# An encoder block in split float32: weights' low part last in each K tile, and two low parts per gate and up product made by an accumulating transfer

## The chip, the cores and the metric

The kernel runs on one core of one Trainium2 chip. The metric is the device time of one execution in microseconds (us), the median of several runs. The engines of a core are TensorE (PE, the matmuls; PEld is its loading of weights), VectorE (DVE), ScalarE (ACT), GpSimd (POOL) and SyncE (SP), which issues most of the transfers. Transfers are carried by 16 DMA engines, whoever issues them.

## The reference

One layer of an encoder for 256 tokens of width 2048, all in float32. What matters here is its last part, the feed-forward block, and that all products are matrix products with weights read from HBM once:

```python
x = x + concatenate([out_mla, out_diff]) @ w_out        # two kinds of attention
...
x = x + xo @ w_xo                                        # cross attention
hf = rms_norm(x, g_ffn)
x = x + (silu(hf @ w_gate) * (hf @ w_up)) @ w_down       # 2048 -> 5632 -> 2048
return rms_norm(x, g_final)
```

## The kernel before

**Split float32.** Each float32 operand is held as two parts, high (`.h`) and low (`.l`), in a type that TensorE takes at its fast rate. A product is three matmuls that add into the same accumulator: high by high, high of the activation by low of the weight, low of the activation by high of the weight. The helper `mm` (lines 97 to 101) issues them in this order, at lines 99, 100 and 101. In it the left operand is the activation, which is loaded as TensorE's weights, and the right one is the model's weight, which streams through. `split_into` (line 105) makes the parts of a weight: ScalarE copies the float32 values into `wh`, which rounds them (line 107), and VectorE subtracts the rounded values from the float32 ones into `wl` (line 108).

**Wide products.** `wide_project` (line 254) computes 256 tokens by 1024 columns: two token tiles (`tt`) by two column halves (`oc`), four accumulators of 128x512. The contraction is cut into pairs of K tiles, 256 deep; gate and up have eight pairs (2048 deep). The weights of a pair are one load of 1 MB into a raw buffer `wraw` (`pair_raw`, line 211, issued on SP at line 214, three buffers). A pair is of one of two kinds:

- a plain pair, `P` (lines 270 to 280): two weight blocks of 128x1024, one for each K tile `k`, each split into `wh` and `wl`, and 8 products, 24 matmuls, written in the order `tt`, `oc`, `k`;
- a summed pair, `W` (lines 284 to 318): a scheme with sums of blocks that needs 7 products, 21 matmuls, instead of 8. VectorE forms sums of weight blocks first (`tsum`, lines 287, 291 and 292), which are split as well. Its results go partly to the four accumulators, partly to four more, `Q`.

The split weights have four buffers of 128x1024 for the high and four for the low parts; a plain pair takes two, a summed pair three (and one of another pool). So ScalarE can split at most about two pairs ahead, and then waits for TensorE to be done with the oldest buffer.

For gate and up the kinds are `GU_KINDS = "PPWPWPWP"` (line 39), so that pairs 2, 4 and 6 are summed. The gate product takes the pairs in the order 0 to 7, the up product in the order 0, 2, 1, 4, 3, 6, 5, 7 (line 41). `wide_result` (line 325) runs one such product; the last step, `join` (line 338), adds each accumulator to what the summed pairs gave, on VectorE (line 340). The accumulators and `Q` have four banks each, and change places after every product (line 322). `wide_chunk` (line 901) does gate, SiLU, up and their product for 1024 hidden columns; there are five such chunks (lines 935 to 942), so ten products by `wide_result`. The same `wide_project` also serves the output projection and the down projection (`wide_add`, line 345), and `mm` serves every other product of the kernel.

**Order.** The program gives the order of dependences; which instruction an engine takes next is fixed when the program is built, by a planner that goes through the work with planned times and gives each engine a list. On the chip each engine runs its list in order, and waits where an operand isn't there. Loads by SP are kept in program order. GpSimd's queue carries small arithmetic, four loads of `mem` (line 807) and, at the end, two loads of the last gain (line 952), issued like all its transfers in the order of its list.

Of the kernel before, what the change touches and what calls it, by code (L numbers as in the profile page):

```python
# [15 lines left out]
AF = mybir.ActivationFunctionType  # L16
ALU = mybir.AluOpType
# [4 lines left out]
NT = S // P  # L22
# [14 lines left out]
NPC = (FF - 512) // 1024  # L37

GU_KINDS = "PPWPWPWP"

G_ORDER, U_ORDER = (0, 1, 2, 3, 4, 5, 6, 7), (0, 2, 1, 4, 3, 6, 5, 7)

# [38 lines left out]
def encoder_block(ctx: ExitStack, tc: tile.TileContext, a, out):  # L81
    nc = tc.nc
# [13 lines left out]

    def mm(o, l, r, start, stop, seeded=False):

        nc.tensor.matmul(o, l.h, r.h, start=start, stop=False, skip_group_check=seeded)  # L99
        nc.tensor.matmul(o, l.h, r.l, start=False, stop=False, skip_group_check=seeded)  # L100
        nc.tensor.matmul(o, l.l, r.h, start=False, stop=stop, skip_group_check=seeded)  # L101

    last_split, last_cast = [None], [None]

# [115 lines left out]
        return Split(*[pool.tile([P, 1024], F32R, name=x, tag=x, bufs=bufs)[:, :n * 512].rearrange(  # L220
            "p (b c) -> p b c", b=n) for x in tags])

    def split_blocks(src, pool=None):
        w = w_tile(src.shape[1], pool)
        split_into(w, src)
        return w

    class Pair:
# [22 lines left out]
        split_into(f[:, 4:8, :], s)  # L251
        return Pair(forms=f)

    def wide_project(pairs, src, order, kinds, leave, join, closed=(0, 1), before=None, seed=None):

        accs = [[acc_tile() for _ in range(2)] for _ in range(NT)]
        used = [[seed is not None] * 2 for _ in range(NT)]
# [7 lines left out]
        for n, i in enumerate(order):  # L265
# [2 lines left out]
                before(n)  # L268
            raw = pair_raw(src[i])
            if i not in summed:  # L270
                w = [split_blocks(raw[:, 2 * k:2 * k + 2, :]) for k in range(2)]
                for tt in range(NT):
                    for oc in range(2):
                        for k in range(2):

                            ends = stop or i == plain[-1] and tt == oc == 1
                            mm(accs[tt][oc], pairs[i].at(k, tt), w[k][:, oc, :], not used[tt][oc],
                               ends and k == 1 and oc in closed, seed is not None)
                            used[tt][oc] = True
                continue  # L280
            if i == summed[0]:
                Q = {q: ps_tile(f"q{q}") for q in (1, 5, 7, 6)}
# [24 lines left out]
            own = i == summed[0], i == summed[-1]  # L307
            t1, t3, t2, t4 = [t[:, j, :] for t in (t13, t24) for j in range(2)] if sum_pool else t13 + t24
            A11, A12, A21, A22, S5, S6, S7, S3 = [pairs[i].forms[:, n, :] for n in range(8)]
            mm(Q[1], A11, b11[:, 0, :], *own)  # L310
            mm(accs[0][1], S3, b11[:, 1, :], False, stop, seed is not None)
            mm(Q[5], S5, t1, *own)
            mm(Q[7], S7, t3, *own)
            mm(accs[0][0], A12, b21[:, 0, :], False, stop, seed is not None)
            mm(Q[6], S6, t2, *own)
            mm(accs[1][0], A22, t4, False, stop, seed is not None)
            if i == summed[-1]:
                leave(Q)
        for tt in range(NT):
# [5 lines left out]
    def wide_result(pairs, src, order, kinds):  # L325

        res = []

        def leave(Q):
            res[:] = [act.tile([P, 2, 512], F32, name=f"res{tt}", tag="act") for tt in range(NT)]  # L330
            q1, x, v, y = res[0][:, 0, :], res[0][:, 1, :], res[1][:, 0, :], res[1][:, 1, :]
            nc.scalar.copy(out=q1, in_=Q[1])
            nc.vector.tensor_tensor(out=v, in0=Q[6], in1=q1, op=ALU.subtract)
            nc.vector.tensor_tensor(out=x, in0=Q[5], in1=v, op=ALU.add)
            nc.vector.tensor_tensor(out=v, in0=v, in1=Q[7], op=ALU.subtract)
            nc.vector.tensor_tensor(out=y, in0=Q[5], in1=v, op=ALU.add)

        def join(tt, oc, acc):
            r = res[tt][:, oc, :]
            nc.vector.tensor_tensor(out=r, in0=acc, in1=r, op=ALU.subtract if (tt, oc) == (1, 0) else ALU.add)  # L340

        wide_project(pairs, src, order, kinds, leave, join)
        return res

    def wide_add(pairs, src, order, kinds, oc0, done=None, closed=(0, 1), before=None):
# [744 lines left out]
```

## Time and profile before

| | |
|---|---|
| median of 3 runs | 1142.07 us (1141.78 to 1142.09) |
| the profiled execution's own time | 1141.65 us |
| its span, first to last instruction | 1139.8 us |
| granted TensorE clock | 0.998 |
| instructions | 14403, of them 5390 matmuls |

The profile is of one execution. Its page has the busy time of each engine; the groups of instructions by line, with count, busy time, mean duration and the idle time ahead of them with what ended it; and the DMA queues. The trace behind it answers further views: waits (engine, line and tile that waited, `<-`, what it waited for, then the sum in us, the number of times and the longest), stretches of time with each engine's busy time, a timeline (start, duration, engine, line, operation, out<-in, shape, and in brackets the idle time before and what ended it), and for a line its instructions and the time from a transfer's issue to its landing, as shortest, median and longest. A matmul's shown duration of 0.39 us is longer than the distance to the next one, since matmuls overlap in the array; the distance between starts is its price.

### The profile page before, as it was taken

The page shows a single profiled execution, that of the slowest core. Times are in us where ns is not written, and L with a number is a line of the kernel's source. Part 1 is how long each engine was busy: PE and PEld are TensorE (multiplying, and loading weights), DVE is VectorE, ACT ScalarE, POOL GpSimd, SP SyncE. Part 2 cuts the span into 40 slices and gives each one's busy share as a digit, 9 for nine tenths or more (in the row PEclk, how much of TensorE's full clock was granted, in tenths as well). Part 3 has the DMA queues.
Part 4 walks back from the last instruction along what each step waited for, and adds up shares of the span by engine and source line. Part 5 has one row for each costly group of instructions (what it writes and reads, how often), then busy time and mean ns, then how long its engine had stood idle before and what let it go on. Part 6 is the DMA issues. An engine that isn't in the chain of part 4 may idle for free.

```text
span 1139.8 us, 14403 instructions
## 1 busy us (share of the span) xinstructions
PE 1130.6 (99%) x5390; PEld 946.4 (83%) x5390; DVE 973.2 (85%) x1322; ACT 667.5 (59%) x965; POOL 58.6 (5%) x75
## 2 busy tenths in 40 slices
PE   9999999999999999999999999999999999999997
PEld 7888888888788888888888888888888888888886
DVE  7788766878896777989898988998998898999895
ACT  7755455567566555665565555565554564665663
POOL 5910000000001000000000000000000000000000
PEclk9999999999999999999999999999999999999999
DMA  9655333546567444455556556556555555565553
GB/s 362 241 195 185 124 125 139 181 149 224 191 227 259 156 161 179 161 211 189 212 194 219 185 191 218 185 190 216 185 187 220 201 205 190 191 247 196 195 181 129
DMA packets 35494, 222.13 MB, mean 195 GB/s; under 512 B 4321, under 2 KB 5601, under 8 KB 11105
## 3 DMA queue, kind: packets, MB, share of 16 engines
q1 hardware_dynamic: 33696, 216.60, 52.9%
q0 software_dynamic: 864, 3.15, 0.8%
q10 hardware_dynamic: 864, 1.47, 0.4%
q8 instruction: 42, 0.69, 0.2%
q14 instruction: 28, 0.22, 0.1%
HBM read 219.11 MB, written 2.10 MB: 194 GB/s over the span
## 4 chain that ended last, share of the span: by engine, by line
PE 98%; issue 1%; ACT 0%; DVE 0%; POOLq 0%; POOL 0%; ACTq 0%
PE acc L99 26%; PE acc L101 26%; PE acc L100 26%; PE q L100 4%; PE q L99 4%; PE q L101 4%; PE pt L502 2%; PE ppt L650 1%; PE psc L100 1%; PE psc L101 1%; PE psc L99 1%; PE acckv L99 0%; PE acckv L101 0%; PE acckv L100 0%; PE pt L922 0%
## 5 line engine op out<-in xcount | busy, mean ns | idle before, releaser
L107 ACT CAST wh<-wraw 128x1024 fp32r<-128x1024 f32 (+2 forms) x401 | 389.8, 989 | 283.2 <-PE acc L101 219.5
L108 DVE TENSOR_TENSOR wl<-wraw,wh 128x1024 fp32r<-128x1024 f32 (+2 forms) x401 | 455.3, 1148 | 88.8 <-ACT wh L107 86.8
L107 ACT CAST wh<-tsum 128x1024 fp32r<-128x1024 f32 (+1 forms) x98 | 98.0, 1006 | 73.1 <-PE acc L101 29.7
L108 DVE TENSOR_TENSOR wl<-tsum,wh 128x1024 fp32r<-128x1024 f32 (+1 forms) x98 | 113.6, 1165 | 19.5 <-ACT wh L107 19.5
L100 PE MATMUL acc<-wl,x2n_h 128*128 128x512 f32 x320 | 124.5, 390 | 0.0
L101 PE MATMUL acc<-wh,x2n_l 128*128 128x512 f32 x320 | 123.9, 389 | 0.0
L99 PE MATMUL acc<-wh,x2n_h 128*128 128x512 f32 x320 | 108.2, 390 | 0.0
L100 PE MATMUL acc<-wl,x0T_h 128*128 128x512 f32 x224 | 88.5, 395 | 0.0
L101 PE MATMUL acc<-wh,x0T_l 128*128 128x512 f32 x224 | 88.2, 394 | 0.0
L99 PE MATMUL acc<-wh,x0T_h 128*128 128x512 f32 x224 | 86.9, 396 | 0.0
L100 PE MATMUL q<-wl,forms_h 128*128 128x512 f32 x191 | 74.3, 389 | 0.0
L101 PE MATMUL q<-wh,forms_l 128*128 128x512 f32 x191 | 74.1, 389 | 0.0
L100 PE MATMUL acc<-wl,hT_h 128*128 128x512 f32 x188 | 73.3, 392 | 0.0
L101 PE MATMUL acc<-wh,hT_l 128*128 128x512 f32 x188 | 72.4, 389 | 0.0
L101 PEld LDWEIGHTS acc<-wh,x2n_l 128*128 128x128 f32 x320 | 60.1, 188 | 12.4
L100 PEld LDWEIGHTS acc<-wl,x2n_h 128*128 128x128 f32 x320 | 60.1, 188 | 12.3
L99 PEld LDWEIGHTS acc<-wh,x2n_h 128*128 128x128 f32 x320 | 59.9, 188 | 12.3
L99 PE MATMUL q<-wh,forms_h 128*128 128x512 f32 x191 | 66.7, 389 | 0.0
L99 PE MATMUL acc<-wh,hT_h 128*128 128x512 f32 x188 | 64.5, 391 | 0.0
L100 PE MATMUL acc<-wl,forms_h 128*128 128x512 f32 x162 | 62.5, 389 | 0.0
L101 PE MATMUL acc<-wh,forms_l 128*128 128x512 f32 x162 | 62.4, 389 | 0.0
L99 PE MATMUL acc<-wh,forms_h 128*128 128x512 f32 x162 | 61.3, 389 | 0.0
(402 smaller groups left out, 2247.9 us busy)
## 6 DMA issues: line engine op xcount, KB each, us to landing
wraw<-in_w_gate SPq DMA_DIRECT2D x44, 1024.0 KB, 4.8
wraw<-in_w_up SPq DMA_DIRECT2D x44, 1024.0 KB, 4.8
wraw<-in_w_dn SPq DMA_DIRECT2D x41, 1024.0 KB, 4.8
wraw<-in_w_in SPq DMA_DIRECT2D x24, 1024.0 KB, 4.8
wraw<-in_w_out SPq DMA_DIRECT2D x16, 1024.0 KB, 4.8
wraw<-in_w_in_lat SPq DMA_DIRECT2D x5, 832.0 KB, 7.2
wraw<-in_w_xk SPq DMA_DIRECT2D x4, 1024.0 KB, 5.4
wraw<-in_w_xq SPq DMA_DIRECT2D x4, 1024.0 KB, 5.9
```

Of the source, the lines that this page charges most:

```text
L99: nc.tensor.matmul(o, l.h, r.h, start=start, stop=False, skip_group_check=seeded)
L100: nc.tensor.matmul(o, l.h, r.l, start=False, stop=False, skip_group_check=seeded)
L101: nc.tensor.matmul(o, l.l, r.h, start=False, stop=stop, skip_group_check=seeded)
L107: last_cast[0] = nc.scalar.copy(out=dst.h, in_=src).ins
L108: last_split[0] = nc.vector.tensor_tensor(out=dst.l, in0=src, in1=dst.h.bitcast(F32), op=ALU.subtract).ins
L502: nc.tensor.transpose(out=pt[:, j * P:(j + 1) * P], in_=src[:, j * P:(j + 1) * P], identity=ident)
L650: nc.tensor.transpose(out=pt[:, kt * S + tt * P:kt * S + (tt + 1) * P], in_=p[:, tt, kt * P:(kt + 1) * P], identity=ident)
```

## The change

Two things are changed. First, the three matmuls of a product now come as high by high, low of the activation by high of the weight, and then high of the activation by low of the weight. A new helper `mm_late` does this for several products at once: for all of them the first two matmuls, and then for all of them the last one. In a plain pair it gets the four products of one K tile at a time, so that `k` is now the outer loop; in a summed pair it gets groups of two, and one single product.

Second, in the gate and up products the second block (`k == 1`) of pairs 1 and 5 gets its low part in another way. ScalarE writes the negated rounded values into `wl` and the rounded values into `wh`; then GpSimd issues a transfer from the raw weights (in SBUF) onto `wl` that adds what it brings to what is there. VectorE's subtraction isn't done for these blocks.

```diff
+GU_CARRIED = (1, 5)
...
     def mm(o, l, r, start, stop, seeded=False):
-        nc.tensor.matmul(o, l.h, r.h, start=start, stop=False, skip_group_check=seeded)
-        nc.tensor.matmul(o, l.h, r.l, start=False, stop=False, skip_group_check=seeded)
-        nc.tensor.matmul(o, l.l, r.h, start=False, stop=stop, skip_group_check=seeded)
+        mm_late([(o, l, r, start, stop)], seeded)
+
+    def mm_late(products, seeded=False):
+        for o, l, r, start, stop in products:
+            nc.tensor.matmul(o, l.h, r.h, start=start, stop=False, skip_group_check=seeded)
+            nc.tensor.matmul(o, l.l, r.h, start=False, stop=False, skip_group_check=seeded)
+        for o, l, r, start, stop in products:
+            nc.tensor.matmul(o, l.h, r.l, start=False, stop=stop, skip_group_check=seeded)
...
-    def split_blocks(src, pool=None):
+    def split_blocks(src, pool=None, by_transfer=False):
         w = w_tile(src.shape[1], pool)
-        split_into(w, src)
+        if by_transfer:
+            nc.scalar.activation(w.l, src, AF.Copy, scale=-1.0)
+            last_cast[0] = nc.scalar.copy(out=w.h, in_=src).ins
+            nc.gpsimd.dma_start(out=w.l, in_=src, accum_op=ALU.add)
+        else:
+            split_into(w, src)
         return w
...
-                w = [split_blocks(raw[:, 2 * k:2 * k + 2, :]) for k in range(2)]
-                for tt in range(NT):
-                    for oc in range(2):
-                        for k in range(2):
+                w = [split_blocks(raw[:, 2 * k:2 * k + 2, :], by_transfer=k == 1 and i in carried) for k in range(2)]
+                for k in range(2):
+                    products = []
+                    for tt in range(NT):
+                        for oc in range(2):
                             ends = stop or i == plain[-1] and tt == oc == 1
-                            mm(accs[tt][oc], pairs[i].at(k, tt), w[k][:, oc, :], not used[tt][oc],
-                               ends and k == 1 and oc in closed, seed is not None)
+                            products.append((accs[tt][oc], pairs[i].at(k, tt), w[k][:, oc, :], not used[tt][oc],
+                                             ends and k == 1 and oc in closed))
                             used[tt][oc] = True
+                    mm_late(products, seed is not None)
                 continue
...
-            mm(Q[1], A11, b11[:, 0, :], *own)
-            mm(accs[0][1], S3, b11[:, 1, :], False, stop, seed is not None)
-            mm(Q[5], S5, t1, *own)
-            mm(Q[7], S7, t3, *own)
-            mm(accs[0][0], A12, b21[:, 0, :], False, stop, seed is not None)
-            mm(Q[6], S6, t2, *own)
-            mm(accs[1][0], A22, t4, False, stop, seed is not None)
+            seeded = seed is not None
+            mm_late([(Q[1], A11, b11[:, 0, :], *own), (accs[0][1], S3, b11[:, 1, :], False, stop)], seeded)
+            mm_late([(Q[5], S5, t1, *own), (Q[7], S7, t3, *own)], seeded)
+            mm(accs[0][0], A12, b21[:, 0, :], False, stop, seeded)
+            mm_late([(Q[6], S6, t2, *own), (accs[1][0], A22, t4, False, stop)], seeded)
...
-        wide_project(pairs, src, order, kinds, leave, join)
+        wide_project(pairs, src, order, kinds, leave, join, carried=GU_CARRIED)
```

More of the change, by code (lines that the diff above doesn't have):

```diff
@@ L252, in summed_pair, with wide_project @@
         return Pair(forms=f)
-    def wide_project(pairs, src, order, kinds, leave, join, closed=(0, 1), before=None, seed=None):
+    def wide_project(pairs, src, order, kinds, leave, join, closed=(0, 1), before=None, seed=None, carried=()):
         accs = [[acc_tile() for _ in range(2)] for _ in range(NT)]
```

## The prediction

> **What bounds the kernel now.** I read the page's totals first, then the waits of TensorE, then the busy time of the gate and up stage, because the transfers that the change adds all lie there.
>
> ```profile
> span 1139.8 us, 14403 instructions
> ...
> PE 1130.6 (99%) x5390; PEld 946.4 (83%) x5390; DVE 973.2 (85%) x1322; ACT 667.5 (59%) x965; POOL 58.6 (5%) x75
> ...
> q1 hardware_dynamic: 33696, 216.60, 52.9%
> q0 software_dynamic: 864, 3.15, 0.8%
> ```
>
> TensorE is busy in all but 9.2 us of the span. A busy TensorE can still stand still for a moment, so the waits have to be seen. The view of waits, for TensorE alone, has three rows in all:
>
> ```profile
> PE wps L384 <- DVE warm L378: 1.2, 1, 1.2
> PE acc L99 <- ACT acc L261: 0.8, 1, 0.8
> PE po L99 <- ACT val_h L113: 0.2, 1, 0.2
> ```
>
> The first is ahead of the warm-up at the very start. In the work proper TensorE waits 0.8 + 0.2 = 1.0 us, and never for a low part of a weight. The busy time by stages says where the other idle time is:
>
> ```profile
> core 0: us, PE busy (x) PEld busy (x) DVE busy (x) ACT busy (x) POOL busy (x), PEclk, DMA share, GB/s
> 436.00:1030.00 594.00, 594.00 (x2662) 492.15 (x2661) 538.57 (x643) 343.05 (x414) 1.53 (x3) 1.00 0.56 200
> 1030.00:1140.00 110.00, 102.78 (x496) 86.48 (x494) 91.31 (x122) 58.14 (x80) 1.12 (x2) 0.98 0.48 172
> ```
>
> From 436 to 1030 us, which holds all gate and up products, TensorE is busy 594.00 of 594.00 us at the full clock. The other 7.2 us (110 less 102.78) are the tail after the last matmul. VectorE is busy 538.57 of the 594, ScalarE 343.05, and neither is waited for. The pace of the matmuls closes the account. These are the first matmul of one gate pair's 24 and the first of the next pair:
>
> ```profile
> 703.18 0.39 PE L99 MATMUL acc<-wh,oddh 128*128 128x512 f32 x1
> ...
> 708.62 0.39 PE L99 MATMUL acc<-wh,x2n_h 128*128 128x512 f32 x1
> ```
>
> 5.44 us for 24 matmuls is 0.227 us each, one behind the other. So the kernel is bound by the number of its matmuls, and the change leaves that number as it is. What can be gained is the 1.0 us of waits; what can be lost is any wait that is put into a stage that has none.
>
> **The change part by part.** *Order of the matmuls.* High by high, low of the activation by high, and only then high by low of the weight; and in plain pairs the first K tile of all four accumulators before the second. The number of matmuls and weight loads stays. A low part is needed later, which spares waits that the view doesn't show: 0, with -1.0 to 0 as bounds; I take -0.3. The order makes all four accumulators of a last plain pair finish in its last four matmuls, 0.9 us, where the written order let one finish every six, 1.36 us apart, so the first joins start up to 4.1 us later. Four joins at 0.68 us are 2.7 us of VectorE; the banks are wanted again by the next product's first summed pair, at the earliest one plain pair (5.4 us) later. That covers it.
>
> *Work removed from VectorE, added to ScalarE.* Five wide chunks, gate and up, two pairs each: 20 subtractions go, 20 negating copies come.
>
> ```profile
> L108 DVE TENSOR_TENSOR wl<-wraw,wh 128x1024 fp32r<-128x1024 f32 x334 | 403.9, 1222 | 78.0 <-ACT wh L107 76.3
> L107 ACT CAST wh<-wraw 128x1024 fp32r<-128x1024 f32 x334 | 345.8, 1052 | 238.1 <-PE acc L101 185.4 <-issue 23.7 <-PE q L101 8.7
> ...
> L340 DVE TENSOR_TENSOR res<-acc,res 128x512 f32<-128x512 f32 x40 | 26.3, 682 | 0.4 <-PE acc L101 0.4
> ```
>
> VectorE loses 20 x 1.22 = 24.4 us. TensorE never waits for it, so that is worth 0. ScalarE gets 20 x 1.05 = 21 us more, and it stands idle for 185.4 us before these casts alone, until TensorE frees a weight buffer. It works in order, so casts behind a negation come 1.05 us later. For an up product's pair 5, these are pair 7's casts:
>
> ```profile
> 675.37 1.99 ACT L107 CAST wh<-wraw 128x1024 fp32r<-128x1024 f32 x2
> ...
> 693.91 1.05 ACT L107 CAST wh<-wraw 128x1024 fp32r<-128x1024 f32 x1 [1.06 <-PE acc L101]
> ...
> 695.34 2.95 ACT L107 CAST wh<-wraw 128x1024 fp32r<-128x1024 f32 x3
> ```
>
> The three casts from 695.34 are pair 5's second block and pair 7's two. They end at 698.29, would end at 699.34, and pair 7's matmuls begin at 703.18: 3.8 us of cover, cost 0.
>
> *The transfer.* This is the term that decides. GpSimd issues it when the negation is done, here at about 695.34 + 1.05 = 696.4. Its low part is wanted by the last four matmuls of the pair, which ends where pair 7 begins, at 703.18; four matmuls before that stands this row (the one above it is used further down):
>
> ```profile
> 691.17 0.84 PE L99 MATMUL q<-wh,forms_h 128*128 128x512 f32 x3
> ...
> 702.28 0.39 PE L100 MATMUL acc<-wl,x2n_h 128*128 128x512 f32 x1
> ```
>
> So it has from 696.4 to 702.28, 5.9 us. That the negation can't start much sooner is seen in the bracket on the cast at 693.91: ScalarE stands waiting for a buffer that TensorE still reads. No accumulating transfer is in the trace. The nearest rows are the two plain loads of the same size, 512 KB, on the same queue (line 807 and line 952):
>
> ```profile
> L807 POOL DMA_DIRECT2D mn<-in_mem x4: 537/543/790, 347.5 to 349.4; - x4
> ...
> DMA to landing us min/median/max: 4.9/6.6/10.1
> ```
>
> ```profile
> L952 POOLq EVENT_SEMAPHORE  x2: 17/21316/42616, 435.7 to 1015.8; - x2
> ...
> DMA to landing us min/median/max: 6.9/7.2/7.6
> ```
>
> Each row is of several loads that share the queue (the four go out within 1.9 us of each other, and 10.1 is the last of them); a carried transfer goes alone, so the shortest, 4.9 us, is nearest, and it reads the on-chip memory instead of HBM. The floor is 512 KB on SP's queue, 3.5 us:
>
> ```profile
> wraw<-in_w_down SPq DMA_DIRECT2D x6, 512.0 KB, 3.5
> ```
>
> Against it: the destination has to be read as well, and weights come in beside it (52.9% of the DMA engines' time). Queue 0's 864 packets for six 512 KB loads took 0.8% of 16 engines, 146 us, which is 144 packets, 9 an engine, and 1.5 us an engine for one load. I take 4.9 and half of that 1.5 more for the second reading, 5.6 us: 0.3 us early. Bounds: 3.5 to 7.6, thus 2.4 early to 1.7 late; early is worth nothing, late costs 0 to 1.7 x 20 = 34 us. The order of TensorE's matmuls is fixed when the program is built, by planned times; it can put other pairs' matmuls ahead of the four, which would widen the 5.9 us, but on the chip it can't change.
>
> By the Trainium skill ("DMA: Bandwidth & Descriptors", section "Anatomy of one DMA — SWDGE (gpsimd) path") such a transfer costs 2.0 us and its bytes at 436 GB/s, an estimate of 3.2 us for 512 KB. By that it would be 2.7 us early; the trace's rows are above it, 4.9 at the least, and they are what the sum uses.
>
> *Issue.* 20 x 0.54 = 11 us on GpSimd, which is busy 58.6 us. The load of line 952 sits at the head of its queue from 435.7 to 1015.8, waiting; the transfers come ahead of it in the program and have to be issued in that time, so that it waits behind them costs nothing before 1015. 20 transfers add 10 MB to 222, 20 MB with the destination's reading.
>
> *The raw buffer.* A transfer reads the raw weights until it lands, and the load three later needs that buffer. SP waits for just this kind of release, a low part's subtraction:
>
> ```profile
> SPq L214 <- DVE wl L108: 645.0, 127, 11.5
> ```
>
> Pair 1 of the same up product:
>
> ```profile
> 678.50 0.33 SPq L214 DMA_DIRECT2D wraw<-in_w_up  x1
> ```
>
> ```profile
> 677.25 1.22 DVE L108 TENSOR_TENSOR wl<-wraw,wh 128x1024 fp32r<-128x1024 f32 x1
> ...
> 685.94 1.22 DVE L287 TENSOR_TENSOR tsum<-wraw 128x1024 f32<-128x1024 f32 x1
> ```
>
> The subtraction ends at 678.47, the load goes at 678.50, and with
>
> ```profile
> wraw<-in_w_up SPq DMA_DIRECT2D x44, 1024.0 KB, 4.8
> ```
>
> it lands at 683.3; its first reader runs at 685.94, 2.6 us later. Pair 1's second cast ran at 675.37 (the negation would take its place, and the transfer go at 676.4), so at 5.6 us the transfer lands at 682.0, the load goes 3.5 us later than 678.50 and its reader is 0.9 us late. From the reader's start a sum (1.22) and a cast (1.05) lead to 688.2; TensorE takes up that summed pair first at 691.17. The 2.9 us between hide the 0.9: cost 0. At 7.6 us the reader is 2.9 us late, just covered. Loads queued on SP behind the held one are held too, by less.
>
> Sum, against the profiled execution's own 1141.65 us (span 1139.8 and 1.85 around it): -0.3 + 0 = 1141.3. That run lies 0.4 under the median of 1142.07, so the forecast for the median is **1141.8 us**, no change that a measurement of this kernel could tell (0.2%, 2.3 us).
>
> **The rivals.** *A, forecast:* transfers land in time. Own range 1140.5 (all waits gone, and 0.5 of scatter) to 1144.3 (a few land a tenth late).
>
> *B, slower: the low part comes late.* The place is the last four matmuls of pairs 1 and 5; it decides from 5.9 us on. For it: but for the 4.9, every time in the two rows is over 5.9. Against: those shared their queue, and the order may have been planned with other matmuls between. At 6.6 us it costs 0.7 x 20 = 14 us, 1156; at 7.6, 34 us, 1176.
>
> *C, slower: every byte is read twice.* The transfer reads source and destination through the same engines, so its 1.5 us an engine doubles: 4.9 + 1.5 = 6.4 at best, up to 7.6 + 1.5 = 9.1, and is 0.5 to 3.2 us late, 10 to 64 us; likeliest near the lower end, 0.65 us late, 13 us, 1155. The Trainium skill says that such an add needs two source reads and pushes twice the traffic through the read ring ("Collectives: The Full Stack", section "The bandwidth ceiling: the fold count and why AG ≠ RS ≠ AR"). No run here shows it yet.
>
> *D, slower: the held raw buffer.* The place is the sums of gate pair 4 and up pair 6, whose load needs the buffer of pair 1; it decides from a transfer of 7.6 us on. At 9.1 us the reader is 4.4 us late against 2.9 of cover, 1.5 us in 10 of the 20 cases, 15 us, 1157. It comes only along with B or C, so little is left for it alone.
>
> *E, faster:* the new order changes the pace of the matmuls, or saves at the start and the tail. 1% of TensorE's 1130.6 us would be 11 us. Against: the trace has the three kinds in several orders, and the pace is 0.227 through all of the 24 above.
>
> **How the numbers follow.** A 0.50, B 0.24, C 0.18, D 0.03, E 0.05. Faster is E, 0.05; same is A, 0.50; slower is B, C and D, 0.45. Likeliest is A, 1141.8. The range begins at A's 1140.5 and goes up to 1164, over B's middle (1159) and C's lower half; left out are E, B's top quarter and C's upper part, about 0.2.
>
> **What would show it.** Right: TensorE's waits stay near 1 us, no row in which its matmuls at the new line for the low part wait for a DMA onto wl, VectorE about 24 us less busy, ScalarE 21 more, 20 transfers on queue 0 landing within 5.9 us of their issue. Wrong by B or C: a row of PE waiting for a DMA onto wl, near 20 times, and landing times above 5.9. Wrong by D: VectorE's sums at the line of tsum waiting for raw weights for more than the few us of now, with TensorE waiting behind. Wrong altogether: gains in stages where TensorE had no wait.

## The result, and the profile after

The changed kernel takes **1153.03 us** (median of 4 runs, 1150.71 to 1154.26), against 1142.08 for the kernel before on the same chip: a ratio of 1.0094, 95% interval 1.0076 to 1.0111. That is 10.9 us slower, where the forecast was no change. The two kernels' runs don't overlap. The time lies inside the range, 2 to 3 us under the likeliest prices of rivals B (1156) and C (1155), but, as the runs below show, mostly for another reason than either.

The totals of the page after (the profiled execution took 1152.62 us):

```profile
span 1150.8 us, 14749 instructions
...
PE 1134.9 (99%) x5390; PEld 947.0 (82%) x5390; DVE 950.3 (83%) x1302; ACT 684.1 (59%) x985; POOL 75.5 (7%) x95
...
q0 software_dynamic: 3744, 13.63, 5.7%
```

The work moved as forecast: the same 5390 matmuls, VectorE 22.9 us less busy, ScalarE 16.6 more (the page counts overlapping instructions once; its 20 copies alone add up to 21.1), 10 MB more on queue 0. TensorE is 4.3 us more "busy" though it does the same, and the span has grown by 11.0: so it both waits more and, somewhere, runs slower. The view of waits for TensorE, all of its rows:

```profile
PE q L106 <- ACT forms_h L115: 2.8, 1, 2.8
PE acc L106 <- ACT wh L115: 2.2, 4, 0.7
PE wps L397 <- DVE warm L391: 1.2, 1, 1.2
PE po L107 <- DVE val_l L122: 1.1, 2, 0.8
PE acc L109 <- DVE wl L116: 0.4, 1, 0.4
PE acc L109 <- DMA wl<-wraw: 0.3, 1, 0.3
PE po L106 <- ACT val_h L121: 0.2, 1, 0.2
```

Leaving the warm-up out, 1.0 us of waits has become 7.0. The surprise is what leads the list. A DMA onto `wl`, which rivals B and C named, is next to last. The longest wait is a single one, for `forms_h`: the activation of a summed pair, in a down product, where no transfer was added. And `val_l` (line 122) belongs to the cross attention, where the change touches nothing but the order of three matmuls.

What follows that longest wait, in the timeline of TensorE:

```profile
583.66 0.39 PE L109 MATMUL acc<-wl,forms_h 128*128 128x512 f32 x1
586.86 0.50 PE L106 MATMUL q<-wh,forms_h 128*128 128x512 f32 x1 [2.81 <-ACT forms_h L115]
...
588.12 0.63 PE L109 MATMUL q<-wl,forms_h 128*128 128x512 f32 x1
588.55 0.63 PE L106 MATMUL q<-wh,forms_h 128*128 128x512 f32 x1
```

From 587.7 to 590.7 the starts are 0.43 us apart instead of 0.227. The busy time by stretches shows why; the third figure from the right is the granted clock:

```profile
580.00:583.60 3.60, 3.60 (x17) 2.98 (x16) 3.60 (x7) 1.86 (x3) 0.00 (x0) 1.00 0.18 30
587.50:590.70 3.20, 3.20 (x10) 2.44 (x9) 1.77 (x2) 2.09 (x2) 0.00 (x0) 0.51 0.82 317
592.00:600.00 8.00, 8.00 (x37) 6.64 (x36) 6.48 (x8) 5.39 (x7) 0.00 (x0) 1.00 0.53 200
```

After the wait the clock stood at half for 3.4 us (the trace's clock records have it from 587.6 to 591.0). So this one wait costs its 3.0 us and 1.7 more. By the Trainium skill ("TensorE: Matmul & The Clock Gate", section "What's actually happening") the clock falls to half after an idle window of about 3.4 us, counted freely, and comes back after as much busy time; the trace agrees with the half and, by these 3.4 us, with the way back, but here 2.8 us of idle time were enough.

Adding up, over all matmuls, how far the distance to the next start exceeds 0.227 us gives 22.1 us after and 12.9 before; the 9.2 between them is most of the loss. By places, after less before:

- 4.7 us at this wait;
- 1.7 at 1068 to 1075 us, behind VectorE's `wl` and `hT_l`;
- 1.7 at two waits for ScalarE's `wh` (762 and 1016 us);
- 1.2 at three waits for the DMA onto `wl` (961, 999 and 1048 us; two of them are too short for a row of the view above);
- 1.2 in the cross attention (403 to 407 us) and 0.4 in the memory projection (328 us);
- 0.7 in the first nine microseconds, long before the first transfer (481 us).

Against these stands 1.0 at 288 us, the prediction's wait for `acc`, which is gone; all other places together have 1.3 less than before.

The transfers themselves, by the view of line 236:

```profile
L236 POOL DMA_DIRECT2D wl<-wraw x20: 854/862/933, 481.2 to 1042.9; - x20
...
DMA to landing us min/median/max: 4.5/4.5/5.5
```

They landed in 4.5 us, at worst 5.5, inside the 5.9 us that were reckoned to be there. But 5.9 was worked out at one place of the 20. Where TensorE stood for a transfer, the low part was wanted sooner: 4.3 us after the issue at 961 us, 4.1 at 999 and 5.4 at 1048.

**Where the long wait comes from.** `forms_h` is made from the product of gate and up. The last four matmuls of an up product, the joins of the four accumulators and the first transposes, here from the timeline of before:

```profile
558.71 1.29 DVE L340 TENSOR_TENSOR res<-acc,res 128x512 f32<-128x512 f32 x2 [0.36 <-PE acc L101]
...
561.00 0.39 PE L101 MATMUL acc<-wh,oddl 128*128 128x512 f32 x1
...
564.86 0.60 PE L502 MATMUL pt<-ident,res 128*128 128x128 f32 x4
...
581.39 0.37 ACT L107 CAST forms_h<-pt 128x256 fp32r<-128x256 f32 x1 [0.67 <-DVE sums L248]
```

and here from the timeline after:

```profile
561.42 1.07 PE L109 MATMUL acc<-wl,oddh 128*128 128x512 f32 x4
...
562.50 2.48 DVE L353 TENSOR_TENSOR res<-acc,res 128x512 f32<-128x512 f32 x4
...
569.36 0.60 PE L515 MATMUL pt<-ident,res 128*128 128x128 f32 x4
...
586.43 0.37 ACT L115 CAST forms_h<-pt 128x256 fp32r<-128x256 f32 x1 [1.64 <-DVE sums L261]
```

The last matmul of the product starts at 561.00 before and at 561.42 + 3 x 0.227 = 562.10 after, so the changed kernel is 1.1 us behind at this point. But its four accumulators are all finished by that one group of four matmuls, so the four joins run in one block from 562.50, 3.8 us later than the first one did before, 2.7 of them not from being behind; the transposes come 4.5 us later, the forms 5.0 (3.9 of them new; the 1.2 beyond the joins' 2.7 arise between joins and forms, and I haven't traced them), and the down product stands.

**Where the late `wl` and `hT_l` come from.** The last transfer took longest, 5.5 us from 1042.92, and landed at 1048.43. SP waited 9.9 us for it, the longest single wait in this row, and sent the load of raw weights that needed its buffer at 1048.57:

```profile
SPq L222 <- DMA wl<-wraw: 164.3, 20, 9.9
```

ScalarE stood for that load and VectorE behind ScalarE; from 1056.60 to 1074.30 VectorE was then busy for 17.62 of 17.70 us, among other things with the block of four joins, and TensorE stood for it:

```profile
1055.49 2.00 ACT L115 CAST wh<-wraw 128x1024 fp32r<-128x1024 f32 x2 [4.92 <-DMA wraw<-in_w_dn]
1056.57 1.23 DVE L116 TENSOR_TENSOR wl<-wraw,wh 128x1024 fp32r<-128x1024 f32 x1 [5.49 <-ACT wh L115]
1070.30 0.49 PE L109 MATMUL acc<-wl,forms_h 128*128 128x512 f32 x1 [0.40 <-DVE wl L116]
```

This is rival D's mechanism, a raw buffer held by a transfer, with a place and a size of its own: the loads behind the last transfer, and 1.7 us.

### The profile page after: what moved, and what is told of

It is laid out like the page before. It is cut to its first block, busy times and chain, and to the rows that moved or that the text cites. A ratio compares the mean times of both kernels' runs of the same rounds, so it can differ in the third digit from the quotient of the medians.

```text
span 1150.8 us, 14749 instructions
## 1 busy us (share of the span) xinstructions
PE 1134.9 (99%) x5390; PEld 947.0 (82%) x5390; DVE 950.3 (83%) x1302; ACT 684.1 (59%) x985; POOL 75.5 (7%) x95
## 4 chain that ended last, share of the span: by engine, by line
PE 86%; DMA 4%; DVE 4%; issue 4%; ACT 1%; SPq 0%; POOLq 0%; POOL 0%; ACTq 0%; DVEq 0%
PE acc L106 23%; PE acc L109 23%; PE acc L107 23%; PE q L107 3%; PE q L106 3%; PE q L109 3%; DVE wl L116 2%; PE pt L515 2%; DMA wl<-wraw 1%; DMA wraw<-in_w_up 1%; DMA wraw<-in_w_dn 1%; PE ppt L663 1%; PE psc L109 1%; PE psc L107 1%; PE psc L106 1%
## 5 line engine op out<-in xcount | busy, mean ns | idle before, releaser
L116 DVE TENSOR_TENSOR wl<-wraw,wh 128x1024 fp32r<-128x1024 f32 (+2 forms) x381 | 431.4, 1145 | 125.9 <-ACT wh L115 102.4
L115 ACT CAST wh<-wraw 128x1024 fp32r<-128x1024 f32 (+2 forms) x381 | 369.5, 985 | 250.9 <-PE acc L107 163.6
L106 PE MATMUL acc<-wh,x2n_h 128*128 128x512 f32 x320 | 125.1, 391 | 0.0
L109 PE MATMUL acc<-wl,x2n_h 128*128 128x512 f32 x320 | 94.0, 391 | 0.4 <-DMA wl<-wraw 0.3
L106 PE MATMUL q<-wh,forms_h 128*128 128x512 f32 x191 | 74.7, 392 | 2.9 <-ACT forms_h L115 2.8
L106 PE MATMUL acc<-wh,hT_h 128*128 128x512 f32 x188 | 72.6, 391 | 0.0
L109 PE MATMUL q<-wl,forms_h 128*128 128x512 f32 x191 | 69.6, 392 | 0.0
L302 DVE TENSOR_TENSOR tsum<-wraw 128x1024 f32<-128x1024 f32 x44 | 53.7, 1220 | 5.6 <-DMA wraw<-in_w_up 2.7
```

Of the source, the lines that this page charges most:

```text
L109: nc.tensor.matmul(o, l.h, r.l, start=False, stop=stop, skip_group_check=seeded)
L115: last_cast[0] = nc.scalar.copy(out=dst.h, in_=src).ins
L116: last_split[0] = nc.vector.tensor_tensor(out=dst.l, in0=src, in1=dst.h.bitcast(F32), op=ALU.subtract).ins
L302: nc.vector.tensor_tensor(out=t[:, 0:2, :], in0=raw[:, 1:3, :], in1=raw[:, 0:1, :].to_broadcast([P, 2, 512]), op=ALU.add)
```

## The experiments

The theory after this reading: most of the loss comes from the order of the matmuls, by two details of it (accumulators that finish together, and the activation's low part being wanted second), and the transfers add a smaller part. The rival: the transfers are what costs, directly, by the raw buffer that they hold, or by ScalarE's copies. The kernel before ran beside each experiment and took 1141.95 to 1142.22 us.

**1. The order alone.** The new order everywhere, no transfers.

```diff
-GU_CARRIED = (1, 5)
+GU_CARRIED = ()
```

> All of the new order of matmuls, no transfer: VectorE makes all low parts again. Order theory (the loss of 11 us comes from the order: accumulators of a plain pair all finish in its last four matmuls, so joins, the product of gate and up, the transposes and the forms of the down product come later, and TensorE waits for forms_h near the down products): 1150 to 1153 us, with the 3 us wait for forms_h still there. Transfer theory (low parts, casts and loads delayed by the transfers): 1141 to 1143 us, and no wait of TensorE over 1 us. If both parts have a share, between 1144 and 1149.

Measured: 1148.72 us (1145.88 to 1149.08), ratio 1.0053 (1.0038 to 1.0068). Its waits of TensorE without the warm-up and `val_h`:

```profile
PE q L106 <- ACT forms_h L115: 2.9, 1, 2.9
...
PE po L107 <- DVE val_l L122: 1.1, 2, 0.8
PE acc L106 <- ACT wh L115: 0.5, 1, 0.5
```

The order alone costs 6.6 us, inside what was expected if order and transfers both have a share, with the waits for `forms_h` and `val_l` of the changed kernel; the transfers are left with 1153.0 - 1148.7 = 4.3. The waits behind VectorE at 1068 to 1075 us are not there, nor is there a row of ScalarE waiting for raw weights of gate, up or `in_w_dn`. The profiled execution took 1145.88 us, and in it the clock stayed at 1.00 through the 3 us after the `forms_h` wait, at a mean of 0.999; the other three took 1148.6 to 1149.1 at a mean of 0.996 to 0.997. So the half clock seems to come after this wait in some executions and not in others; only the profiled ones show it directly.

**2. The transfers alone.** The order of before, in all products, with the 20 transfers.

```diff
-                w = [split_blocks(raw[:, 2 * k:2 * k + 2, :]) for k in range(2)]
+                w = [split_blocks(raw[:, 2 * k:2 * k + 2, :], by_transfer=k == 1 and i in carried) for k in range(2)]
                 for tt in range(NT):
                     for oc in range(2):
                         for k in range(2):
```

> The kernel before with its own order of matmuls, and the 20 transfers. Order theory: 1142 to 1143 us, since a transfer lands in 4.5 us and the time it has is 5.9; at most the 0.9 us of waits for transfers that the changed kernel shows. Transfer theory: 1149 us or more, rather above the changed kernel, since the low part is wanted earlier in a pair. Only-together theory: 1142 to 1143 here and in the run with the order alone.

Measured: 1169.56 us (1168.4 to 1170.2), ratio 1.024 (1.0223 to 1.0257). The first rows of TensorE's waits, and the transfers:

```profile
PE acc L102 <- DMA wl<-wraw: 12.9, 11, 2.2
PE q L101 <- ACT forms_h L109: 2.8, 2, 1.8
```

```profile
wl<-wraw POOLq DMA_DIRECT2D x20, 512.0 KB, 4.5
```

The order theory's 1142 to 1143 fell. Here is the wait that rivals B and C described: the transfers take the same 4.5 us in the median, but the low part is wanted by the fifth matmul of the pair instead of the last four. So the two halves of the change belong together: without the late order the transfers cost 27 us. The waits in these two rows come to 15.7 of the 27; three stretches of 3.4 us at half the clock add some 5, and I have not accounted for the rest row by row.

**3. and 4. The two parts of the order.** First, without transfers, only the three matmuls of a product turned round, with loops and grouping as before:

```diff
         nc.tensor.matmul(o, l.h, r.h, start=start, stop=False, skip_group_check=seeded)
-        nc.tensor.matmul(o, l.h, r.l, start=False, stop=False, skip_group_check=seeded)
-        nc.tensor.matmul(o, l.l, r.h, start=False, stop=stop, skip_group_check=seeded)
+        nc.tensor.matmul(o, l.l, r.h, start=False, stop=False, skip_group_check=seeded)
+        nc.tensor.matmul(o, l.h, r.l, start=False, stop=stop, skip_group_check=seeded)
```

> Only the three matmuls of each product in the new order (high by high, low of the activation by high, high by low of the weight), for every product of the kernel; the loops of a plain pair as before (token tile, column half, K tile), no grouping, no transfers. Order theory with the loops as the cause: 1141.5 to 1142.5 us, accumulators finish one by one. If the order of the three is the cause: 1147 to 1153. Transfer theory: 1142.

Measured: 1144.4 us (1143.56 to 1145.48), ratio 1.002 (1.0011 to 1.003), with the wait for `val_l` and none for `forms_h`. Then only the loops of a plain pair turned round, K tile outermost, with the three matmuls as before:

```diff
-                for tt in range(NT):
-                    for oc in range(2):
-                        for k in range(2):
+                for k in range(2):
+                    for tt in range(NT):
+                        for oc in range(2):
```

> Only the loops of a plain pair changed, K tile outermost; the three matmuls of a product in the old order, no grouping, no transfers. Order theory with the loops as the cause: 1147 to 1153 us, with a wait of TensorE for forms near the first down product. If the order of the three or the grouping is the cause: 1141.5 to 1142.5. Transfer theory: 1142.

Measured: 1145.1 us (1144.11 to 1146.97), ratio 1.0028 (1.0016 to 1.004). Here the longest wait is the other one, and `val_l` is gone from the list:

```profile
PE q L99 <- ACT forms_h L107: 2.5, 1, 2.5
```

Each half of the order has its own wait. Both times lie between the two values that had been expected, since neither half is the whole cause: 2.3 and 3.0 us make 5.3 of the 6.6.

**5. and 6. Mending one detail at a time in the changed kernel.** First the end of a product: its last pair goes in the loops of before, one product at a time; all else, transfers too, as in the changed kernel.

```diff
-                for k in range(2):
-                    products = []
-                    for tt in range(NT):
-                        for oc in range(2):
...
-                    mm_late(products, seed is not None)
+                places = [(k, tt, oc) for k in range(2) for tt in range(NT) for oc in range(2)]
+                if stop:
+                    places = [(k, tt, oc) for tt in range(NT) for oc in range(2) for k in range(2)]
...
+                for n0 in range(0, 8, 1 if stop else 4):
+                    mm_late(products[n0:n0 + (1 if stop else 4)], seed is not None)
```

> The changed kernel, but in the last pair of each wide product the loops are as before (token tile, column half, K tile), one product at a time, so that accumulators finish one by one. Late-accumulator theory: the 3 us wait for forms_h near the first down product goes, and with it up to 1.6 us of half clock behind it: 1147.5 to 1150.5 us. Rival (any reordering of matmuls costs this much, wherever the accumulators end): 1152 to 1155, with the wait there or at another place.

Measured: 1147.47 us (1145.87 to 1147.94), ratio 1.0045 (1.003 to 1.006). The wait for `forms_h` has left the list, and 5.6 of the 10.9 us with it. The waits behind VectorE at 1068 to 1075 us are gone as well, though ScalarE waits 5.2 us for the held load here too: three of the four joins run before it, and no longer in one block behind it. Then, instead, single products (the helper `mm`) in the order of before, groups as in the changed kernel:

```diff
     def mm(o, l, r, start, stop, seeded=False):
-        mm_late([(o, l, r, start, stop)], seeded)
+        nc.tensor.matmul(o, l.h, r.h, start=start, stop=False, skip_group_check=seeded)
+        nc.tensor.matmul(o, l.h, r.l, start=False, stop=False, skip_group_check=seeded)
+        nc.tensor.matmul(o, l.l, r.h, start=False, stop=stop, skip_group_check=seeded)
```

> The changed kernel, but every single product (attention, projections by pieces, one product of each summed pair) has its three matmuls in the old order; only the grouped ones have the low part of the weight last. Theory: the attention's output products, whose left operand's low part is wanted second instead of third, lose 1.3 us near 404 us and the memory projection 0.3: 1151 to 1152 us, with the waits for val_l there gone. Rival (the place is planned by chance): 1153 and the waits stay or move.

Measured: 1150.9 us (1150.17 to 1152.42), ratio 1.008 (1.0065 to 1.0095): 2.1 us come back, and `val_l` has left the list, as has the 0.4 in the memory projection. (The two kernels' runs overlap; runs 7 and 12 give 2.2 for the same edit without transfers, where they don't.) Why that wait arises is seen in the cross attention. The product with the values is called with `val` as the left operand, so the reversed order wants `val_l` second instead of third. Before:

```profile
404.80 0.28 PE L99 MATMUL po<-pxT_h,val_h 128*128 128x256 f32 x1
404.92 0.28 PE L100 MATMUL po<-pxT_l,val_h 128*128 128x256 f32 x1
405.24 0.39 PE L101 MATMUL po<-pxT_h,val_l 128*128 128x256 f32 x1
```

After:

```profile
404.27 0.50 PE L106 MATMUL po<-pxT_h,val_h 128*128 128x256 f32 x2 [0.16 <-ACT val_h L121]
405.06 0.39 PE L107 MATMUL po<-pxT_h,val_l 128*128 128x256 f32 x1 [0.28 <-DVE val_l L122]
...
405.79 0.50 PE L106 MATMUL po<-pxT_h,val_h 128*128 128x256 f32 x2
407.12 0.38 PE L107 MATMUL po<-pxT_h,val_l 128*128 128x256 f32 x1 [0.83 <-DVE val_l L122]
```

**7. Both details mended, no transfers.** What is left of the change is the grouping: weights' low parts last in each K tile of all wide products, but for their last pair.

> The last two edits together, and no transfer. If late accumulators and the order of single products are all that the order costs: 1141.5 to 1143.5 us. If grouping as such costs as well: 1145 to 1148.

Measured: 1141.8 us (1141.6 to 1142.33, 10 runs), ratio 0.9999 (0.999 to 1.0008). The order's whole cost is gone. Neither does the grouping gain anything.

**8. The transfer reads HBM instead of the raw buffer.** In the changed kernel, so that no transfer holds a raw buffer.

```diff
-            nc.gpsimd.dma_start(out=w.l, in_=src, accum_op=ALU.add)
+            nc.gpsimd.dma_start(out=w.l, in_=by_transfer, accum_op=ALU.add)
...
-                w = [split_blocks(raw[:, 2 * k:2 * k + 2, :], by_transfer=k == 1 and i in carried) for k in range(2)]
+                w = [split_blocks(raw[:, 2 * k:2 * k + 2, :], by_transfer=src[i][:, 2:4, :] if k == 1 and i in carried else None) for k in range(2)]
```

> The changed kernel, but the transfer reads the raw weights from HBM a second time, instead of from the raw buffer; the buffer is free as soon as ScalarE has read it. Held-buffer theory (the 4.3 us that the transfers add to the order come from loads of raw weights issued about 4 us later): 1148 to 1150.5 us, SP waits for wl transfers gone, ScalarE no longer waiting for raw weights of up, gate and down. Rival (they come from transfers' own lateness, or from ScalarE's 20 more copies): 1152 to 1155, above the changed kernel if reading HBM makes the transfer slower.

Measured: 1194.58 us (1186.99 to 1196.72), ratio 1.0447 (1.0405 to 1.0488). The expectation for the held buffer fell; what came is what the rival had named at its end, a slower transfer: this edit changes the transfer's own time far more than the buffer. Its transfers, and the leading waits of TensorE:

```profile
wl<-in_w_gate POOLq DMA_DIRECT2D x10, 512.0 KB, 8.3
wl<-in_w_up POOLq DMA_DIRECT2D x10, 512.0 KB, 8.4
```

```profile
PE acc L109 <- DMA wl<-in_w_up: 26.2, 10, 5.5
PE acc L109 <- DMA wl<-in_w_gate: 6.3, 7, 2.1
```

So it answers nothing about the held buffer, but it tests the 5.9 us: landing after 8.3 to 8.4 is 2.4 to 2.5 too late, which 20 times makes 48 to 50 us by rival B's sum; against the changed kernel it lost 41.6. That this is near is in part luck. The two rows hold 17 waits of 32.5 us in all, and half the clock for 23.9 us of the span gives some 12 more. Taking each wait off its transfer's time to landing, the low part was wanted 5.3 to 7.1 us after the issue in the up products and 6.3 or more in the gate products. So the point from which a transfer is late was about right for the up products, and too early for the gate ones.

**9. Both details mended, transfers kept.** Single products as in run 6, the last pair of a product as in run 5.

> The changed kernel with both edits at once: the last pair of each wide product one product at a time, and single products in the written order of before; the 20 transfers stay. Without the transfers this order takes 1141.8 us. If order and transfers cost independently of each other, the transfers leave what they added before (1153.0 - 1148.7 = 4.3 us): 1146.1, and 1150.9 - (1153.0 - 1147.5) = 1145.4 by the two other runs. If most of what the transfers cost comes only by way of the waits that the order makes (a long wait of TensorE and the slower matmuls behind it), it is 1142.5 to 1144. The view of waits tells which: a DMA onto wl, or ScalarE's and VectorE's wh and wl behind a raw buffer that came late.

Measured: 1143.92 us (1143.46 to 1145.0, 11 runs), ratio 1.0017 (1.0008 to 1.0026). Its waits of TensorE without the warm-up and `val_h`:

```profile
PE acc L101 <- ACT wh L117: 1.0, 2, 0.5
PE acc L111 <- DMA wl<-wraw: 0.9, 1, 0.9
```

The transfers cost 2.1 us over run 7 (1.9 when each is taken against the kernel before that ran beside it), half of the 4.3 that they cost in the changed kernel: the two parts are not independent, as the second expectation had it. Of the two waits for `wh`, one lies at 7.5 us, before any transfer, and the other is run 7's. In this kernel the one wait for a DMA belongs to the one transfer that took longest, 6.2 us, the last, which shares queue 0 with the loads of the last gain. With two shorter ones (535 and 702 us) the distances at waits for the DMA are 1.6 us too long, so in this execution the late low part is most of what can be seen. ScalarE still waits 4.9 us for the held load, as in the changed kernel, but here TensorE never stands behind it.

**10. The negated copies alone.** As run 9, but the low parts are VectorE's, and nothing uses ScalarE's 20 copies.

```diff
         if by_transfer:
             nc.scalar.activation(w.l, src, AF.Copy, scale=-1.0)
-            last_cast[0] = nc.scalar.copy(out=w.h, in_=src).ins
-            nc.gpsimd.dma_start(out=w.l, in_=src, accum_op=ALU.add)
-        else:
-            split_into(w, src)
+        split_into(w, src)
```

> As the last, but the low parts are VectorE's subtraction again and no transfer is issued; ScalarE still writes the 20 negated copies, which nothing uses. Theory that the transfers cost by their lateness or by the raw buffer that they hold: no loss here, 1141.5 to 1142.5. Rival, that the 21 us of ScalarE are not free, since casts of later pairs come late: most of the 4 us is here, 1144.5 to 1146, with TensorE waiting for ScalarE's wh.

Measured: 1143.19 us (1142.8 to 1143.59), ratio 1.0009 (1.0 to 1.0018). The only rows beside `val_h` and the warm-up:

```profile
PE acc L101 <- ACT wh L117: 1.2, 3, 0.5
```

Between the two expectations: 1.4 us over run 7 (1.1 when each is taken against the kernel before beside it), with two new waits for ScalarE of 0.3 us each, at 755 and 1008 us. Run 3, which has no copies, has waits at the same two places, and run 9, which has them, has none there; so it may be the new list of the planner as much as the copies.

**11. The transfers without their use.** With a tile of its own for the negated copy the buffers no longer fit on the chip: a pool of 16.06 KB per partition would have had 13.72 left. So, as run 10, but the negated copy goes over the first half of the raw buffer, after that half has been split, and the transfer goes onto it; TensorE waits for no transfer.

```diff
         split_into(w, src)
+        if over is not None:
+            nc.scalar.activation(over, src, AF.Copy, scale=-1.0)
+            nc.gpsimd.dma_start(out=over, in_=src, accum_op=ALU.add)
```

> Order as in the kernel with both edits. The low parts are VectorE's subtraction; after the second cast of a carried pair ScalarE writes the 20 negated copies over the first half of the raw buffer, which has been split by then, and the accumulating transfer reads the second half and goes onto the first. So copies, issue, traffic and the held raw buffer are there (held about 1 us longer than in the changed kernel), but TensorE waits for no transfer. Both edits without transfers took 1141.8, with the copies alone 1143.2, with the transfers used 1143.9. Theory that what the transfers add to the copies is the late low part: 1142.8 to 1143.5, and no wait of TensorE for a DMA. Rival, that it is the raw buffer held: 1143.9 or more, with casts behind raw weights that came late.

Measured: 1151.05 us (1149.71 to 1154.48), ratio 1.0084 (1.0071 to 1.0098). That is 7 us above run 9, which the theory did not allow; but the edit held the buffer longer than I had reckoned. One place, first in run 9:

```profile
711.57 0.86 POOL L238 DMA_DIRECT2D wl<-wraw  x1 [12.72 <-ACT wl L236]
...
721.35 1.22 DVE L305 TENSOR_TENSOR tsum<-wraw 128x1024 f32<-128x1024 f32 x1
```

and then in run 11, which was abreast of run 9 until then (the sum before this one starts at 710.62 us, in run 9 at 710.67):

```profile
715.57 0.87 POOL L238 DMA_DIRECT2D wraw<-wraw  x1 [16.37 <-ACT wraw L237]
...
720.20 2.48 SPq L224 DMA_DIRECT2D wraw<-in_w_gate  x2
...
727.11 1.23 DVE L303 TENSOR_TENSOR tsum<-wraw 128x1024 f32<-128x1024 f32 x1 [4.06 <-DMA wraw<-in_w_gate]
...
728.45 1.21 DVE L118 TENSOR_TENSOR wl<-wraw,wh 128x1024 fp32r<-128x1024 f32 x1
```

```profile
729.72 1.65 PE L111 MATMUL acc<-wl,x2n_h 128*128 128x512 f32 x3 [2.58 <-DVE wl L118]
```

The copy had to wait for VectorE, the transfer went at 715.57, 4.0 us later than in run 9, and the raw weights were released at 720.20. The sum at 727.11 then waited 4.06 us for its load, the subtraction stood behind it on VectorE, and TensorE behind that. This is rival D's mechanism again, now with the wait where D put it, in `tsum`, a few microseconds of holding away from the changed kernel. So this run can't divide run 9's rest between the late low part and the held buffer.

**12. One detail mended, no transfers.** Run 5 without its transfers.

> The changed kernel without transfers and with the last pair of each wide product one product at a time; single products keep their low weight last. Order alone took 1148.7, with both edits 1141.8. Theory that the late accumulators of a product's end cost about 4.5 us by the chain to the down product, and the order of single products about 2.3 us by the low part of val: 1143.8 to 1144.6, no wait for forms_h, waits for val_l of 1.1 us. Rival, that the two work together (either edit alone removes little or nearly all): 1142 to 1143 or over 1146.

Measured: 1144.03 us (1143.38 to 1145.51, 11 runs), ratio 1.0019 (1.001 to 1.0028). With runs 1 and 7 this divides the order's cost: 1148.7 - 1144.0 = 4.7 us for the end of the products, 1144.0 - 1141.8 = 2.2 for the single products, as expected. A wait for `forms_h` of 0.2 us is left, which had been expected to go. Against run 5 it gives a third price of the transfers, 1147.5 - 1144.0 = 3.4, with the ends mended and the single products late.

## Why the prediction was wrong

The account in one line: 10.9 us = 4.7 (accumulators that finish together) + 2.2 (single products) + 4.3 (transfers, which cost 2.1 where the other two are absent), less 0.3 by which the kernel before differed from run 7. The parts depend on the order in which they are taken away: with the transfers kept, the two details are worth 9.1 together (run 9), without them 6.9.

- **What bounds the kernel: right.** The number of matmuls does. Run 7 stands at the time of before, and VectorE's lighter load, 22.9 us, bought nothing.
- **The order of the matmuls: this step failed**, and with it the forecast. It took -0.3 us and the runs show +6.6 to +6.9. It failed twice. "A low part is needed later, which spares waits" holds for the weight's low part; of the three matmuls the activation's low one moved up from third to second, and in the cross attention it is the late one. And of the joins, up to 4.1 us later, it said that "the banks are wanted again by the next product's first summed pair ... That covers it". The joins did come later, by 2.7 us of their own, and no bank was missed. But a join has two kinds of followers: whoever needs the bank, and whoever needs the result. The cover was worked out for the first alone. The second is the chain join, product with the gate, transpose, forms, first matmul of a summed pair of the down product; it had less than the 3.9 us to spare by which the forms came late. The rows of that chain behind the joins stood in the trace of before, and the prediction follows none of them.
- **Work from VectorE to ScalarE: nearly right.** 20 copies of 1.056 us by their group, expected 1.05; by run 10 they cost 1.4 us at most, not 0.
- **The transfer: right in the sign, with the wrong working.** 5.6 us was expected, 4.5 measured (5.5 at worst), inside the 5.9. But the 5.9 of one place stood for all 20: three low parts were wanted within 4.1 to 5.4 us, which cost 1.2 us, and run 8 finds 5.3 to over 8. The estimate worked out from the Trainium skill ("DMA: Bandwidth & Descriptors", section "Anatomy of one DMA — SWDGE (gpsimd) path"), 3.2, was too low by 1.3. What was added for the second reading was too little: queue 0's share went from 0.8% of 16 engines over 1139.8 us to 5.7% over 1150.8, which is 904 us for 2880 packets, 0.31 us a packet against 0.17 before, so 2.8 us an engine for a transfer against 1.5. That fits rival C's premise, bytes read twice, but doesn't show it: the page counts 10.5 MB for the 20 transfers, the bytes once, and the source differs too. (The section of the Trainium skill that the prediction cites for it, in "Collectives: The Full Stack", speaks of the adding step of a ReduceScatter; that it holds for a transfer within one core's memory is the prediction's own step.) Rival C's conclusion failed, because the rest of the 4.9 us did not stay: 4.5 - 2.8 leaves 1.7 for all but the data, where 4.9 - 1.5 had left 3.4. That a source on the chip is why is likely, since with HBM as source the same transfer takes 8.3 at the same packet time (queue 0's share is 5.4% of 1191.9 us in run 8).
- **Issue: too small, without consequence.** 0.86 us on GpSimd for each, not 0.54.
- **The held raw buffer: cost 0 was wrong as well.** The cover was worked out for pair 1 alone. Casts of gate, up and `in_w_dn` weights wait 28.6 us on ScalarE for loads that came late, where the kernel before and run 1 have no such row (runs 7 and 10, also without transfers, have 1.7 and 4.0 us). Most of it is hidden; behind the last transfer, in the block of joins, TensorE loses 1.7 us, and as much in run 6, but not in runs 5 and 9, whose joins come one by one, nor in run 1, which has no transfers. Run 11 shows the price once the transfer goes 4 us later.
- **The rivals.** None of them names the main part of what happened, though the time is near those of B and C: TensorE lost 1.2 us at waits for the DMA where B and C put 13 to 14, and 1.7 behind a held buffer where D put 15. Two things were left out of all of them: a path that begins with a result instead of a buffer, and that a wait of 3 us may be followed by 3 us or more at half the clock.

Why the transfers cost more beside the late ends is in part the held buffer: in the profiles its 1.7 us come only where both are there (by the medians, 4.3 against 3.4, it is 0.9, on runs that spread over 2 us and more). Another 1.3 (3.4 less 2.1) goes with the late single products, and that I have not traced. What stays open besides is how the transfers' last 2.1 us divide: run 9 shows 1.6 at late low parts, but run 10, with the copies alone, was 1.4 us slower than run 7, with new waits at places where run 9 has none. Another raw buffer, which would take the holding away, was not tried.

## What to carry to other kernels

When an order is turned round so that one operand may come late, ask which operand now comes early, and list for every result that finishes later both its followers: who needs its buffer and who needs its value. Follow the second to the next point where the bounding engine takes it up; in a kernel with 1 us of waits in all, a delay of 4 us can find a place where it isn't covered, as it did here. A transfer that is too slow for its place can still fit where the reader is moved to the end of its group, as here: 27 us without that, 2.1 to 4.3 with it.

## What the runs showed of the hardware

- An accumulating transfer of 512 KB from SBUF onto SBUF took 4.5 us from issue to landing in the median (at most 5.5 in the changed kernel, 8.1 in run 2), from HBM 8.1 to 10.8, and GpSimd 0.86 us each; its packets took 0.31 us, where those of plain loads from HBM on the same queue took 0.17.
- Around the end of TensorE waits of 2.5 to 2.8 us the granted clock fell to half for 3.4 us (the changed kernel and runs 4 and 11) or 6.8 (run 6); in another execution, after 2.9 us in the same place (run 1), it stayed at 1.00. The kernel of run 1, which has this wait, went from 1145.88 to 1149.08 us over four executions; that of run 7, which hasn't, from 1141.6 to 1142.33 over ten.
